# A macaron hybrid layer on one core: which blocks ask for a modulation column, how far behind the request its sum stands, and where readers of small transfers stand

## The chip, the cores and the metric

One of the eight cores of one Trainium2 chip runs the whole program. The metric is the device time of one execution in microseconds (us), as the median of several runs; lower is better. Beside it stands one execution taken by the hardware profiler. In its rows PE is TensorE (matmul), PEld its weight loads, DVE VectorE, ACT ScalarE, POOL GpSimd, and SP the engine whose queue (SPq) issues every DMA of this kernel. L140 is line 140 of the kernel before.

## The reference, cut

```
mod = silu(c) @ ada_w + ada_b                       # 9 x 2048 numbers: sh1, sc1, gt1, ... gt3
h = ada_in(x, norm_g[0], sh1, sc1);  x = x + 0.5 * gt1 * swiglu(h, gate[0], up[0], down[0])
h = ada_in(x, norm_g[1], sh2, sc2);  x = x + gt2 * hybrid_mixer(h, w_in, w_out, ...)
h = ada_in(x, norm_g[2], sh3, sc3);  x = x + 0.5 * gt3 * swiglu(h, gate[1], up[1], down[1])
return rmsnorm(x, final_norm)

def ada_in(x, g, shift, scale): return rmsnorm(x, g) * (1 + scale) + shift
def swiglu(h, wg, wu, wd):      return (silu(h @ wg) * (h @ wu)) @ wd
```

There are 256 tokens of width 2048 and a hidden width of 5632 = 44 x 128. The mixer has eight attention heads with a forget gate ("fox") and eight heads of a gated delta rule ("gdn") in chunks of 64, behind one input projection. Everything is float32.

## The kernel before, in words

**The weight stream.** All weights lie in device memory as 5392 tiles of 128x128, in the order in which the program uses them, eight to a block: 674 blocks of 512 KB, numbered 0 to 673. Each tile is used once. For each block `Stream.block` (L117) issues the DMA of `wraw` on SP (L125) and lets ACT copy it, rounded, to `whi` (L128); `Stream.next` (L130) lets DVE subtract to get `wlo` (L140). TensorE multiplies with both halves, so that a product is carried by two or three matmuls (L489/L490, L493/L494, L573 to L575). `whi` and `wlo` have four buffers each. `wraw` has four, and within the two feed-forward parts every fifth block goes to a fifth one (`more`), so that there the transfer of block b waits for the `wlo` of block b-5.

**The stages.** Blocks 0 to 111: gate and up products of the first 28 hidden chunks, in pieces (`gate_up_first`, L536); at the end of a chunk DVE adds two halves (L591, L592), multiplies (L524) and splits (L508). Blocks 112 to 167: the down products of those chunks, 3.5 blocks for each of 16 output chunks, with the residual on DVE (L517, L518). Blocks 168 to 231 and 232 to 263: the same for the other 16 hidden chunks. Blocks 264 to 409: the mixer. Blocks 410 to 673: the second feed-forward part.

**The columns.** `mod` has 144 columns of 128 numbers. For each, `ada_col` (L242) issues a DMA of 1 MB (`adat`, L261) placed behind the last `wraw` issue on SP, and DVE multiplies it with `silu(c)` and sums it up (L265; a column's sum, in the trace a custom instruction). `adat` has two buffers and, in the feed-forward parts, a third, so that column i waits for the sum of column i-3 there. The table `RATE` says how many columns each block asks for from a given block on; before, 0.2 in blocks 66 to 111, 0.5 in 112 to 167, 0.38 in 168 to 263, 0 in 264 to 283, 0.255 in 284 to 375, 0 in 376 to 423 and 0.16 after that.

**What sets the order.** Tile's scheduler decides at build time in which order an engine's instructions stand, by its own estimate of when each is ready; it moves an instruction ahead of others where it sees fit. `tc.issue_after(i)` (a pin) makes the instructions under it stand behind instruction i. Each engine then works through its row in that order, and a waiting instruction holds up all behind it. Where `W.late` holds (before: from the mixer on), a column's sum isn't written at once: it is kept in `W.owing`, and `settle` (L109) writes it in a later block under a pin behind that block's `wlo`, `BEHIND` = 2 blocks after the request. `ada_need` (L275), which makes sure that a column is there before it is read, writes all that is owed at once, with no pin. It is called for every tile of `gate_up_first` and once per output chunk in the residuals.

**Small transfers in the mixer.** `gates` stores 16 rows of cumulated gate values to device memory (`rowd`), and they are read back spread over all partitions: four rows at a time to `x<-rowd` (L921) for `decays` (L929, then eight exponentials L932), one row at a time to `rw<-rowd` (L897) for `decay` (`dec`, L908) and for `fox` (`fm`, L1174). `solve` sends blocks through device memory (L989 to L1012) and reads them at L1015 (`U0`). `keys` (L955) lets TensorE write `pk` and `pkk` (L961, L964), three buffers for both, of which `pk` is freed by the copy L968 on ACT and `pkk` by L974 on DVE, which needs the exponentials of L932.

## Time and profile before

| what | value |
|---|---|
| median of 3 runs | 1947.27 us (1946.34 to 1947.93) |
| profiled execution, its own time | 1948.17 us |
| its span, first to last instruction | 1946.4 us |
| PE busy | 1900.8 us, 98% of the span |
| DVE busy | 1558.7 us, 80% |
| ACT busy | 1040.3 us, 53% |
| mean granted TensorE clock | 0.994 |
| moved by DMA | 519.58 MB, mean 267 GB/s |

The profiled execution took 0.90 us more than the median of the runs; what is worked out from its rows is set against its own time, 1948.17 us. A busy PE is the bound of nearly all of the span, so that time can only come from the stretches where PE has no work and from those where its granted clock is below 1. Tables of stretches give, for each, the busy time and the instructions of each engine, the granted clock, the busy share of the DMA engines and GB/s.

### The profile page before, as it was taken

How to read it: one execution, taken by the hardware profiler on the slowest of the kernel's cores; microseconds unless marked ns; L12 is line 12 of the kernel's file. 1: busy time of each engine (PE TensorE's matmuls, PEld its weight loads, DVE VectorE, ACT ScalarE, POOL GpSimd, SP SyncE). 2: the span in 40 equal slices, each digit the busy share in tenths (PEclk: the TensorE clock that was granted, in tenths of full speed). 3: DMA queues.
4: the chain of work that ended last, by engine and by line, in shares of the span. 5: the costliest groups of instructions: out<-in, count | busy, mean ns of one | idle time of the engine just before them, and what ended most of it. 6: DMA issues, size and time to landing. Idle time of an engine off the chain costs nothing.

```text
span 1946.4 us, 33719 instructions
## 1 busy us (share of the span) xinstructions
PE 1900.8 (98%) x13086; PEld 1773.9 (91%) x13087; DVE 1558.7 (80%) x2414; ACT 1040.3 (53%) x1645; POOL 56.8 (3%) x55
## 2 busy tenths in 40 slices
PE   8999998999999999999999999999999999999998
PEld 7999998888899988899989999999999999999997
DVE  6999977999999997789987988877777666666654
ACT  7444544433444445857657656665554345554553
POOL 0000000000000021000000002000000000000011
PEclk9999999999999999999999999999999999999999
DMA  9998876999998885687667557677777666666663
GB/s 383 346 359 332 309 259 241 393 386 378 353 354 352 341 333 200 219 294 244 221 232 266 171 184 238 210 264 266 263 263 267 229 201 200 204 198 202 201 201 120
DMA packets 129490, 519.58 MB, mean 267 GB/s; under 512 B 18217, under 2 KB 21545, under 8 KB 111153
## 3 DMA queue, kind: packets, MB, share of 16 engines
q1 hardware_dynamic: 129330, 517.42, 74.0%
q8 instruction: 103, 1.69, 0.3%
q14 instruction: 57, 0.47, 0.1%
HBM read 512.89 MB, written 4.47 MB: 266 GB/s over the span
## 4 chain that ended last, share of the span: by engine, by line
PE 75%; DVE 11%; DMA 5%; issue 5%; ACT 3%; SPq 0%; DVEq 0%; ACTq 0%
PE pd L493 14%; PE pg L489 10%; PE pu L489 10%; PE pd L494 7%; PE pu L490 5%; PE pg L490 5%; DVE wlo L140 4%; PE po L493 3%; DMA adat<-in_ada_dram 2%; PE pgu L575 2%; PE pgu L573 2%; PE pgu L574 2%; PE pp L796 2%; PE pp L797 2%; PE pp L798 2%
## 5 line engine op out<-in xcount | busy, mean ns | idle before, releaser
L140 DVE TENSOR_TENSOR wlo<-wraw,whi 128x1024 fp32r<-128x1024 f32 x674 | 821.0, 1225 | 256.1 <-ACT whi L128 254.8
L128 ACT CAST whi<-wraw 128x1024 fp32r<-128x1024 f32 x674 | 698.9, 1046 | 504.4 <-PE pd L493 150.9
L493 PE MATMUL pd<-hid,whi 128*128 128x512 f32 x1408 | 462.0, 382 | 0.0
L494 PE MATMUL pd<-hid,wlo 128*128 128x256 f32 x1408 | 384.7, 273 | 4.8 <-DVE wlo L140 4.8
L265 DVE CUSTOM_DVE_ANT_0 adat<-adat,cs,colt 128x2048 f32<-128x2048 f32 x142 | 334.9, 2359 | 22.6 <-DMA adat<-in_ada_dram 22.6
L489 PE MATMUL pg<-hs,whi 128*128 128x512 f32 x912 | 302.3, 382 | 0.5 <-DVE shc L440 0.5
L489 PE MATMUL pu<-hs,whi 128*128 128x512 f32 x912 | 302.1, 382 | 0.0
L493 PEld LDWEIGHTS pd<-hid,whi 128*128 128x128 f32 x1408 | 266.0, 189 | 36.8
L494 PEld LDWEIGHTS pd<-hid,wlo 128*128 128x128 f32 x1408 | 270.2, 192 | 8.2 <-DVE wlo L140 8.0
L575 PE MATMUL pgu<-hs,wlo 128*128 128x256 f32 x896 | 240.6, 278 | 14.7 <-DVE wlo L140 14.3
L490 PE MATMUL pu<-hs,wlo 128*128 128x256 f32 x912 | 249.1, 273 | 0.0
L490 PE MATMUL pg<-hs,wlo 128*128 128x256 f32 x912 | 249.1, 273 | 0.0
L573 PE MATMUL pgu<-hs,whi 128*128 128x256 f32 x896 | 244.9, 277 | 0.4 <-ACT whi L128 0.3
L574 PE MATMUL pgu<-hs,whi 128*128 128x256 f32 x896 | 244.4, 276 | 0.0
L489 PEld LDWEIGHTS pg<-hs,whi 128*128 128x128 f32 x912 | 172.4, 189 | 24.8 <-ACT shc L439 0.7
L489 PEld LDWEIGHTS pu<-hs,whi 128*128 128x128 f32 x912 | 172.4, 189 | 23.7
L796 PE MATMUL pp<-hs,whi 128*128 128x256 f32 x656 | 188.9, 289 | 1.1 <-ACT hs L380 1.1
L575 PEld LDWEIGHTS pgu<-hs,wlo 128*128 128x128 f32 x896 | 168.4, 193 | 18.4 <-DVE wlo L140 18.3
L797 PE MATMUL pp<-hs,whi 128*128 128x256 f32 x656 | 182.4, 278 | 0.0
L798 PE MATMUL pp<-hs,wlo 128*128 128x256 f32 x656 | 181.9, 277 | 0.0
L490 PEld LDWEIGHTS pu<-hs,wlo 128*128 128x128 f32 x912 | 175.0, 192 | 1.0 <-DVE wlo L140 0.9
L490 PEld LDWEIGHTS pg<-hs,wlo 128*128 128x128 f32 x912 | 175.1, 192 | 0.6
(334 smaller groups left out, 2581.4 us busy)
## 6 DMA issues: line engine op xcount, KB each, us to landing
wraw<-in_w_dram SPq DMA_DIRECT2D x674, 512.0 KB, 4.5
adat<-in_ada_dram SPq DMA_DIRECT2D x142, 1024.0 KB, 7.5
xr<-in_xr_dram SPq DMA_DIRECT2D x4, 512.0 KB, 5.4
adaf<-in_ada_dram SPq DMA_DIRECT2D x4, 512.0 KB, 8.3
xd<-x SPq DMA_DIRECT2D x4, 512.0 KB, 7.4
rw<-rowd SPq DMA_DIRECT2D x16, 128.0 KB, 4.3
x<-xd SPq DMA_DIRECT2D x4, 512.0 KB, 5.3
out_dram<-o SPq DMA_DIRECT2D x8, 256.0 KB, 2.7
```

Of the source, the lines that this page charges most:

```text
L128: self.cast = self.nc.scalar.copy(self.h, r).ins
L140: lo_ = nc.vector.tensor_tensor(self.l, r, self.h.bitcast(F32), ALU.subtract)
L265: V.tensor_tensor_reduce(t, t, cs, 1.0, L("adab", q, 1), ALU.mult, ALU.add, mod[:, q : q + 1])
L489: PE.matmul(ps, wt[0], both, start=(k == 0), stop=False)
L490: PE.matmul(ps[:, T:], wt[1], part(k, HI), start=False, stop=(k == KD - 1))
L493: PE.matmul(ps, wt[0], act.rearrange("p q (a b) -> p q b a", a=2), start=first, stop=False)
L494: PE.matmul(ps[:, :T], wt[1], woven(act[:, 0]), start=False, stop=last)
L573: PE.matmul(o, wh, part(k, HI), start=first and s == 0, stop=False, skip_group_check=skip)
L574: PE.matmul(o, wh, part(k, LO), start=False, stop=False, skip_group_check=skip)
L575: PE.matmul(o, wl, part(k, HI), start=False, stop=last, skip_group_check=skip)
L796: PE.matmul(pp[i][:, :T], wh, hh, start=(k == 0), stop=False)
L797: PE.matmul(pp[i][:, :T], wh, hl, start=False, stop=False)
```

## The change

There are four parts:
- `RATE`: no column is asked for in blocks 90 to 111; 0.4 in place of 0.38 in blocks 168 to 263, and 0.285 in place of 0.255 in blocks 284 to 375.
- `W.late` holds from block 66 on (`LATE`), and the sum is settled three blocks after the request up to the mixer (`BEHIND[0]`), then two as before.
- `dec`, the first instruction of `decays`, and `U0` get a pin behind the `wlo` of the block that is current where they are written (`W.split`); the two `fm` instructions get one behind its cast (`W.cast`).
- `decays(1)` (the second four heads) is written 10 units of the planner's clock after it is due to start and not 5.

```diff
-RATE = (... (66, 0.2), (112, 0.5), (168, 0.38), (264, 0.0), (284, 0.255), (376, 0.0), (424, 0.16))
+RATE = (... (66, 0.2), (90, 0.0), (112, 0.5), (168, 0.4), (264, 0.0), (284, 0.285), (376, 0.0), (424, 0.16))
-BEHIND = 2
+BEHIND = (3, 2)
+LATE = 66
...
+            self.late = b >= LATE
...
             with self.tc.issue_after(lo_.ins):
-                self.settle(b - BEHIND)
+                self.settle(b - self.lag)
+            self.split = lo_.ins
...
-            V.tensor_tensor(dd, bc(C("mU")), gbv, ALU.add)
+            with tc.issue_after(W.split):
+                V.tensor_tensor(dd, bc(C("mU")), gbv, ALU.add)
...
-            yield 5.0
+            yield 10.0 if half else 5.0
...
-            V.tensor_tensor(Ln[:, hs4].rearrange("p h t j -> p (h t) j"), mL, rv, ALU.subtract)
+            with tc.issue_after(W.split):
+                V.tensor_tensor(Ln[:, hs4].rearrange("p h t j -> p (h t) j"), mL, rv, ALU.subtract)
...
             for q in range(2):
-                V.tensor_tensor(
+                with tc.issue_after(W.split):
+                    V.tensor_tensor(
...
-                A.activation(fm[:, o : o + wd], cb[:, :wd], AF.Identity, bias=colS[:, t, 0, h : h + 1], scale=-1.0)
+                with tc.issue_after(W.cast):
+                    A.activation(fm[:, o : o + wd], cb[:, :wd], AF.Identity, bias=colS[:, t, 0, h : h + 1], scale=-1.0)
...
-        W.late = True
+        W.lag = BEHIND[1]
```

**Where the columns stand now.** Counted in the order of SP and DVE of both kernels, block by block: in blocks 90 to 111 the kernel before asks for five columns (behind the transfers of blocks 90, 95, 100, 105 and 110), and the changed one for none. Blocks 112 to 167 have 28 in both. Blocks 168 to 263 have 34 before and 37 now, and blocks 264 to 375 have 24 before and 26 now. Before block 87 no column's request or sum has moved, although `W.late` holds from block 66 on: there `ada_need` settles what is owed before every pair of tiles. In blocks 112 to 167 most sums still stand in the block of their request, some one or two blocks later; from block 168 to 230 each stands three blocks later: the requests behind the transfers of blocks 168, 170, 173, 175 and 178 have their sums behind the `wlo` of blocks 171, 173, 176, 178 and 181, where before the requests of blocks 167, 170, 172, 175 and 178 had theirs behind the `wlo` of the same blocks.

DVE in blocks 91 to 95, first before (the first row is the `wlo` of block 91), then now (the rows of the same blocks).

```order
L140 TENSOR_TENSOR wlo<-wraw,whi 128x1024
L524 TENSOR_TENSOR tu<-tu,tg 128x256
L508 TENSOR_TENSOR hid<-tu,hid 128x256
L140 TENSOR_TENSOR wlo<-wraw,whi 128x1024
L265 ISA adat,mod<-adat,cs,colt 128x2048
L265 ISA mod 128x1
L591 TENSOR_TENSOR tg<-pgu,acc 128x256
L592 TENSOR_TENSOR tu<-pgu,acc 128x256
L140 TENSOR_TENSOR wlo<-wraw,whi 128x1024
L524 TENSOR_TENSOR tu<-tu,tg 128x256
L140 TENSOR_TENSOR wlo<-wraw,whi 128x1024
```

```order
L142 TENSOR_TENSOR wlo<-wraw,whi 128x1024
L527 TENSOR_TENSOR tu<-tu,tg 128x256
L511 TENSOR_TENSOR hid<-tu,hid 128x256
L142 TENSOR_TENSOR wlo<-wraw,whi 128x1024 x2
L594 TENSOR_TENSOR tg<-pgu,acc 128x256
L595 TENSOR_TENSOR tu<-pgu,acc 128x256
L527 TENSOR_TENSOR tu<-tu,tg 128x256
L142 TENSOR_TENSOR wlo<-wraw,whi 128x1024
L511 TENSOR_TENSOR hid<-tu,hid 128x256
L142 TENSOR_TENSOR wlo<-wraw,whi 128x1024
```

The sum (the rows ISA) that stood between `wlo` of block 92 and `wlo` of block 93 is gone, and the evacuation of a hidden chunk (tg, tu) stands one block further back. The sum's request stands behind the transfer of block 95 on SP, so that the sum stood three blocks ahead of the block of its own request.

SP where the mixer's rows come back, from the transfer of block 283 on, first before, then now.

```order
L883 DMA rowd<-x 8x512
L125 DMA wraw<-in_w_dram 128x1024
L261 DMA adat<-in_ada_dram 128x2048
L921 DMA x<-rowd 128x4x256
L897 DMA rw<-rowd 128x256 x2
L125 DMA wraw<-in_w_dram 128x1024 x4
L261 DMA adat<-in_ada_dram 128x2048
```

```order
L886 DMA rowd<-x 8x512
L126 DMA wraw<-in_w_dram 128x1024 x2
L925 DMA x<-rowd 128x4x256
L900 DMA rw<-rowd 128x256 x2
L126 DMA wraw<-in_w_dram 128x1024
L264 DMA adat<-in_ada_dram 128x2048
L126 DMA wraw<-in_w_dram 128x1024 x4
```

The read of the four rows (`x<-rowd`) has moved from behind the transfer of block 284 and a column's 1 MB to behind the transfer of block 285 with no column ahead of it.

ACT at the same place, from the cast of block 284 on, first before, then now.

```order
L128 CAST whi<-wraw 128x1024
L949 ACTIVATE kk<-cv 128x256
L1074 ACTIVATE kbd<-kk,colS 128x128
L1174 ACTIVATE fm<-rw,colS 128x128
L1174 ACTIVATE fm<-rw,colS 128x256
L945 COPY cp<-pp 128x256
L967 ACTIVATE j_9065,ssk<-pk 128x128
L932 ACT_TABLE_LOAD
L932 ACTIVATE Ln<-Ln,colS 128x128 x8
L967 ACTIVATE j_9067,ssk<-pk 128x128
L968 COPY kk<-pk 128x256
```

```order
L129 CAST whi<-wraw 128x1024
L1080 ACTIVATE kbd<-kk,colS 128x128
L937 ACT_TABLE_LOAD
L937 ACTIVATE Ln<-Ln,colS 128x128 x8
L954 ACT_TABLE_LOAD
L954 ACTIVATE kk<-cv 128x256
L972 ACTIVATE j_9059,ssk<-pk 128x128
L972 ACTIVATE j_9061,ssk<-pk 128x128
L973 COPY kk<-pk 128x256
L950 COPY cp<-pp 128x256
```

The two `fm` instructions no longer stand ahead of the eight exponentials `Ln`; they now stand behind the cast of block 302. On DVE the subtraction that feeds `Ln` (L929) has moved from behind `wlo` of block 284 to behind `wlo` of block 283, with three short instructions between, and `dec` from block 284 to block 305. From the cast of block 306 to that of block 307 ACT now has a table load, both `dec`, the fox exponentials, all eight `Ln`, a 384-wide copy, a convolution's first two steps and `rw`; before, the eight `Ln` stood behind the cast of block 304 and most of the others behind that of block 307.

More of the change, by code (lines that the diff above doesn't have):

```diff
@@ L34 @@
 NEG = -1e30
[L36 removed]
+RATE = ((0, 0.5), (28, 0.25), (33, 0.5), (49, 0.25), (56, 0.5), (66, 0.2), (90, 0.0), (112, 0.5), (168, 0.4), (264, 0.0), (284, 0.285), (376, 0.0), (424, 0.16))
 N_BIG, N_GDN = 3, 3
@@ L105, in __init__ @@
         self.lead = None
-        self.late, self.owing = False, []
+        self.late, self.owing, self.lag = False, [], BEHIND[0]
     def settle(self, upto=N_TILES):
@@ L1014, in solve @@
             for q in range(2):
-                V.tensor_tensor(
-                    U0[:, hs4].rearrange("p h t (b i) -> p (h t) b i", b=4)[:, 4 * q : 4 * q + 4],
-                    U[:, 4 * q : 4 * q + 4].unsqueeze(2).to_broadcast([P, 4, 4, 16]),
-                    C("blk").unsqueeze(1).unsqueeze(3).to_broadcast([P, 4, 4, 16]), ALU.mult)
+                with tc.issue_after(W.split):
+                    V.tensor_tensor(
+                        U0[:, hs4].rearrange("p h t (b i) -> p (h t) b i", b=4)[:, 4 * q : 4 * q + 4],
+                        U[:, 4 * q : 4 * q + 4].unsqueeze(2).to_broadcast([P, 4, 4, 16]),
+                        C("blk").unsqueeze(1).unsqueeze(3).to_broadcast([P, 4, 4, 16]), ALU.mult)
             if half == 0:
```

1 line of the change is left out of this document (removed).

## The prediction

> **What bounds the kernel now.** I read the page first, then the table of 20 us stretches, and in it looked only for stretches where PE is idle or its clock is below 1.
>
> ```profile
> PE 1900.8 (98%) x13086; PEld 1773.9 (91%) x13087; DVE 1558.7 (80%) x2414; ACT 1040.3 (53%) x1645; POOL 56.8 (3%) x55
> 260.00:280.00 20.00, 20.00 (x182) 20.00 (x181) 12.22 (x17) 8.65 (x11) 0.00 (x0) 1.00 0.70 255
> 280.00:300.00 20.00, 16.64 (x145) 16.26 (x143) 15.22 (x22) 7.70 (x12) 0.00 (x0) 0.98 0.56 194
> 300.00:320.00 20.00, 19.04 (x158) 18.85 (x158) 15.97 (x28) 10.35 (x17) 0.00 (x0) 0.93 0.68 235
> 320.00:340.00 20.00, 17.22 (x154) 17.03 (x153) 16.93 (x29) 10.64 (x17) 0.00 (x0) 1.00 0.72 261
> ```
>
> In each row: the stretch, its length, then busy us (instructions) of PE, PEld, DVE, ACT and POOL, the granted clock, the DMA share and GB/s. PE is the bound, with 1948.17 - 1900.8 = 47 us at most to win. Between 280 and 340 it has 3.36 + 0.96 + 2.78 = 7.1 us without work, while DVE is not full and the DMA engines are at 0.56 to 0.72: nothing there is short of capacity, so something waits for an order. The rows of PE with idle time ahead of them (in brackets, with what ended it) say for what:
>
> ```profile
> 283.21 0.38 PE L575 MATMUL pgu<-hs,wlo 128*128 128x256 f32 x1 [1.29 <-DVE wlo L140]
> 298.94 0.38 PE L575 MATMUL pgu<-hs,wlo 128*128 128x256 f32 x1 [2.07 <-DVE wlo L140]
> 315.19 0.38 PE L575 MATMUL pgu<-hs,wlo 128*128 128x256 f32 x1 [0.96 <-DVE wlo L140]
> 331.64 0.38 PE L575 MATMUL pgu<-hs,wlo 128*128 128x256 f32 x1 [2.78 <-DVE wlo L140]
> 344.16 0.38 PE L494 MATMUL pd<-hid,wlo 128*128 128x256 f32 x1 [1.54 <-DVE wlo L140]
> ```
>
> Five waits for `wlo`, 1.29 + 2.07 + 0.96 + 2.78 + 1.54 = 8.64 us. And DVE, in the rows that lead to the second one:
>
> ```profile
> 289.75 1.23 DVE L140 TENSOR_TENSOR wlo<-wraw,whi 128x1024 fp32r<-128x1024 f32 x1 [0.52 <-ACT whi L128]
> 294.73 2.35 DVE L265 CUSTOM_DVE_ANT_0 adat<-adat,cs,colt 128x2048 f32<-128x2048 f32 x1 [3.76 <-DMA adat<-in_ada_dram]
> 297.01 0.08 DVE L265 DVE_READ_ACCUMULATOR2_ANT mod<- 128x1 f32 x1
> 297.01 0.42 DVE L591 TENSOR_TENSOR tg<-pgu,acc 128x256 f32<-128x256 f32 x1
> 297.35 0.41 DVE L592 TENSOR_TENSOR tu<-pgu,acc 128x256 f32<-128x256 f32 x1
> 297.68 1.22 DVE L140 TENSOR_TENSOR wlo<-wraw,whi 128x1024 fp32r<-128x1024 f32 x1
> ```
>
> After a `wlo` DVE stands still for 3.76 us until the column's megabyte has landed, sums for 2.28 us (297.01 - 294.73), and only then does the evacuation and the next `wlo`, 7.9 us after the last one. The order puts the sum three blocks ahead of its own request's block; the request can't go out before the transfer that it stands behind gets a buffer, and the megabyte then takes 5.4 to 8.3 us:
>
> ```profile
>   DMA adat<-in_ada_dram: 10.3, 3
> DMA to landing us min/median/max: 5.4/7.9/8.3
> ```
>
> (of the columns between 285 and 345, where three of four sums waited).
>
> **The change part by part.**
>
> *No columns in blocks 90 to 111.* Five sums go from there with their waits. The first four gaps each follow one of them; the fifth follows the next column's sum, at 338.58 among the last evacuations, for which DVE had no lead left. Its place is now taken by a sum behind `wlo` of block 112, which DVE meets with its full lead. Without these sums DVE's load per block at its densest (a chunk of hidden values to 1 1/4 blocks, then to one) is a `wlo` of 1.22 us and 0.8 to 1 of a chunk's four short rows at 0.34 start to start, 2.3 to 2.6 us, where PE uses a block in 2.64 us (182 matmuls in 20 us in the row of 260, 24 to a block). So PE has nothing to wait for, though with little to spare over the last four blocks: -8.64 us, of which the last 1.54 may stay.
>
> *The clock.* PE's clock falls right behind the second gap:
>
> ```profile
> 294.00:300.00 6.00, 3.93 (x33) 3.74 (x31) 5.27 (x7) 1.16 (x3) 0.00 (x0) 0.95 0.32 127
> 300.00:310.00 10.00, 10.00 (x79) 10.00 (x79) 6.62 (x12) 6.31 (x9) 0.00 (x0) 0.86 0.86 299
> ```
>
> It costs 0.05 x 6 + 0.14 x 10 = 1.7 us. It begins at the end of a gap, so I let it go with the gap: -1.7 us. This is weaker: the longer gap at 331.64 has no such fall behind it (the row of 320 shows 1.00). [...]
>
> *The mixer's small readers.* One stop there follows from them:
>
> ```profile
> 812.58 0.80 ACT L1174 ACTIVATE fm<-rw,colS 128x128 f32<-128x128 f32 x2 [2.80 <-DMA rw<-rowd]
> 815.22 2.44 ACT L932 ACTIVATE Ln<-Ln,colS 128x128 f32<-128x128 f32 x8
> 816.35 0.44 PE L961 MATMUL pk<-colt,kk 128*128 128x128 f32 x2 [1.13 <-DVE Ln L974]
> 818.22 1.22 PE L964 MATMUL pkk<-kk 128*128 128x128 f32 x4 [1.22 <-ACT kk L968]
> 816.00:820.00 4.00, 2.43 (x9) 2.04 (x10) 2.17 (x10) 4.00 (x16) 0.00 (x0) 0.78 0.58 242
> 820.00:824.00 4.00, 4.00 (x16) 3.34 (x15) 4.00 (x9) 3.87 (x5) 0.00 (x0) 0.80 0.25 74
> ```
>
> ACT waits 2.80 us for a row of 128 KB whose `fm` nobody uses before block 302, and behind it stand the exponentials that free PE's buffers. With `fm` moved to block 302 the exponentials can begin some 3 us earlier. The subtraction ahead of them on DVE now stands behind `wlo` of block 283, and its data comes from a read issued at 802.1 and landed after 8.1 us:
>
> ```profile
> 802.14 0.43 SPq L921 DMA_DIRECT2D x<-rowd  x1
> DMA to landing us min/median/max: 8.1/8.1/8.1
> ```
>
> The order now puts no column of 1 MB ahead of that read, so that it lands at 810.2 or before; DVE may still wait for it a little, which the next `wlo` bears, since it stands some three blocks ahead of PE. The `pk` wait (1.13) then goes; of the `pkk` wait, which hangs on the copy behind a second table load, I keep 0.5. That is -1.85 us, bounds 0 and -2.35. The fall of the clock behind the stop, 0.22 x 4 + 0.20 x 4 = 1.7 us, I let go too.
>
> *Three columns more in blocks 168 to 263.* A sum takes 2.36 us of DVE:
>
> ```profile
> L265 DVE CUSTOM_DVE_ANT_0 adat<-adat,cs,colt 128x2048 f32<-128x2048 f32 x142 | 334.9, 2359 | 22.6 <-DMA adat<-in_ada_dram 22.6
> 345.00:430.00 85.00, 84.36 (x513) 76.80 (x512) 81.03 (x96) 35.96 (x37) 0.00 (x0) 1.00 0.99 395
> 430.00:505.00 75.00, 73.33 (x443) 66.36 (x442) 69.19 (x78) 26.74 (x28) 0.00 (x0) 1.00 0.97 372
> 505.00:590.00 85.00, 85.00 (x519) 77.89 (x518) 78.17 (x91) 42.93 (x65) 0.00 (x0) 1.00 0.93 356
> 680.00:700.00 20.00, 19.68 (x121) 17.85 (x120) 19.60 (x27) 8.61 (x12) 6.58 (x4) 1.00 0.86 339
> 700.00:720.00 20.00, 19.39 (x119) 17.56 (x118) 18.87 (x25) 9.07 (x12) 5.46 (x3) 1.00 0.97 374
> ```
>
> Blocks 168 to 231 run from about 500 to 670, with PE full, 6.8 us of 85 free on DVE and 7% free on the DMA engines: three sums of 7.1 us and 3 MB over 250 us hide there. The cover is gone in the down products (680 to 720), where PE already lost 0.32 + 0.61 = 0.93 us with about six columns (40 us, 2.6 a block, 0.38 a block), 0.16 a column: +0.5 us for three. Bounds 0 and +7.1 (nothing hidden). Blocks 112 to 167 (345 to 505) keep their 28 columns, the DMA at 0.97 to 0.99 and PE's loss of 0.64 + 1.67 = 2.3 us, which may go either way by that much.
>
> *Two columns more in blocks 284 to 375, and the other pins.* Between 860 and 1160 PE is without work for 300 - 292.82 = 7.2 us, in short stops behind chains through DVE and ACT:
>
> ```profile
> 860.00:1160.00 300.00, 292.82 (x2355) 280.98 (x2354) 257.82 (x636) 199.79 (x449) 0.43 (x2) 1.00 0.65 225
> L265 DVE CUSTOM_DVE_ANT_0 adat<-adat,cs,colt x20: 2335/2345/2349, 865.6 to 1136.3; 128x2048 f32<-128x2048 f32 x20
> ```
>
> If they all came of the 20 sums there, a sum would be worth 7.2 / 20 = 0.4: +0.8 us for two, bounds 0 and +4.7 (two sums of 2.35 in full). The other pins move readers further back; each new order of these chains may make or take single stops, -3 to +3 us, and I take 0.
>
> The sum: 1948.17 - 8.64 - 1.7 - 1.85 - 1.7 + 0.5 + 0.8 = 1935.6 us for an execution like the profiled one. That one stood 0.90 us above the median of its runs, so for the median 1934.7 us.
>
> **The rivals.**
>
> *The mixer keeps its stops.* ACT now has between the casts of blocks 306 and 307 the eight exponentials (2.44 us above), a table load of 1.28, and `dec`, the fox rows, the copy and the convolution at 0.4 to 0.5 each, some 8 us in all, where the lead of four `whi` buffers is about three blocks of 2.7 us less a cast and a `wlo`, 5.8 us (both are estimates from the rows of these groups). Where the stretch is not met by a full lead, PE waits for 2.2 us and more, and a stop at 816 that only shifts (1.85 + 1.7) comes on top: 1934.7 + 2.2 + 3.55 = 1940.5. For it speaks that the order has these rows in one piece; against it that PE has small matmuls of the attention in between, which stretch its blocks.
>
> *The clock falls anyway.* If the two falls don't come of the gaps, 3.4 us stay: 1938.1.
>
> *The held buffers starve the transfers: slower.* From block 168 to 230 a column's buffer is freed three blocks later. The request behind the transfer of block 175 needs the buffer of a column whose sum stands behind `wlo` of block 171, while that transfer itself went out after `wlo` of block 170: SP stands for a block and a sum, 2.6 + 2.3 us, and holds up all later transfers, on every second column, once in five blocks or 13 us. In those it must bring 5 x 0.524 + 2 x 1.049 = 4.7 MB. If the engines run dry for 2.5 us of each, the rest takes 4.7 MB in 10.5 us, 449 GB/s, and the trace never shows more than
>
> ```profile
> 20.00:40.00 20.00, 18.73 (x159) 18.09 (x160) 16.89 (x19) 14.92 (x26) 0.00 (x0) 1.00 1.02 423
> ```
>
> over 20 us. By 423 GB/s a cycle takes 11.1 + 2.5 = 13.6 us, 0.6 more than PE; at the 356 of this stage 15.7, 2.7 more. Twelve such cycles cost 8 to 33 us: at the upper end 1934.7 + 33 = 1968. It decides from the point at which nothing is left in flight while SP stands. Against it: when `wlo` is late, four transfers of blocks ahead are still in flight, over 5 us of work, so the engines don't run dry just when it matters, and 363 GB/s (4.7 in 13) is what the stage of 345 exceeded.
>
> *It doesn't do what it says.* The three blocks don't apply from 66 to 90, where the order hasn't changed, nor in most of blocks 112 to 167, where the residuals settle first. No gap of PE hangs on it (the row of 260 has PE at 20.00), so the time is that of the forecast.
>
> **How the numbers follow.** Forecast 0.60, mixer keeps its stops 0.16, clock falls anyway 0.10, starved transfers 0.10, better than 1929 (the 2.3 us of blocks 112 to 167 and half of the mixer's 7.2 go too) 0.04. The range of the forecast with its bounds: down 2.3 and 3, to about 1929; up with the rival of 1940.5 and a further 3 of the mixer's order, to 1944. A measurement of this kernel can tell about 0.2%, 3.9 us, from no change. Faster by more than that means below 1943.4: all cases but the starved one, 0.9; the starved one reaches from 1942.7 (8 us) to 1968: within the bound 0.03, slower 0.07.
>
> **What would show it.** Right: no gap of PE for `wlo` between 275 and 345, no wait of a sum for its megabyte there, the down products beginning some 10 us earlier, no clock below 1 from 290 to 310; at the second stop in the mixer no `pk` wait; SP waiting for a sum of DVE now and then from 490 to 660 with PE still full. Wrong: gaps for `wlo` there or in the down products of blocks 112 to 167, or a stretch of ACT at blocks 306 and 307 with PE idle behind it.

## The result and the profile after

| | median, us | range | runs |
|---|---|---|---|
| before | 1948.18 | 1945.38 to 1953.45 | 21 |
| after | 1950.92 | 1947.94 to 1953.33 | 21 |

The ratio is 1.0013, with a 95% interval of 1.0006 to 1.0020: the change made the kernel slower by a little over a tenth of a per cent. The forecast was 1934.7 us, in a range of 1929 to 1944. The profiled execution after took 1949.35 us, with a span of 1947.5 us (before: 1948.17 and 1946.4).

First the place that the forecast was about, in the same table of 20 us stretches, of the kernel after (stretch, length, then busy us and instructions of PE, PEld, DVE, ACT, POOL, the granted clock, the DMA share and GB/s):

```profile
280.00:300.00 20.00, 20.00 (x182) 20.00 (x181) 13.65 (x21) 9.40 (x14) 0.00 (x0) 1.00 0.59 193
300.00:320.00 20.00, 20.00 (x182) 20.00 (x181) 17.00 (x31) 11.99 (x19) 0.00 (x0) 1.00 0.61 207
320.00:340.00 20.00, 20.00 (x165) 19.55 (x164) 18.79 (x35) 11.72 (x20) 0.00 (x0) 1.00 0.85 318
```

The five gaps are gone, and so is the fall of the clock. So the gain came, and was given back elsewhere. Longer stretches of both kernels show where. Before:

```profile
420.00:500.00 80.00, 77.91 (x468) 70.16 (x467) 74.21 (x84) 28.34 (x27) 0.00 (x0) 1.00 0.98 377
500.00:660.00 160.00, 159.96 (x972) 146.16 (x971) 146.10 (x170) 81.34 (x122) 0.00 (x0) 1.00 0.91 353
660.00:740.00 80.00, 79.07 (x479) 71.79 (x478) 76.72 (x96) 38.39 (x51) 17.51 (x12) 1.00 0.86 318
780.00:860.00 80.00, 77.48 (x494) 70.63 (x493) 66.00 (x150) 59.41 (x107) 0.00 (x0) 0.98 0.69 243
```

After:

```profile
420.00:500.00 80.00, 74.70 (x441) 66.03 (x440) 67.51 (x79) 29.26 (x30) 0.00 (x0) 1.00 0.89 351
500.00:660.00 160.00, 156.27 (x940) 141.23 (x939) 140.63 (x165) 78.29 (x118) 0.00 (x0) 1.00 0.89 349
660.00:740.00 80.00, 76.34 (x452) 67.81 (x451) 78.72 (x97) 34.73 (x45) 16.76 (x11) 1.00 0.89 326
780.00:860.00 80.00, 79.52 (x529) 73.43 (x529) 63.92 (x146) 56.56 (x101) 0.00 (x0) 1.00 0.72 256
860.00:1160.00 300.00, 291.47 (x2339) 280.44 (x2338) 262.72 (x646) 202.67 (x454) 0.42 (x2) 0.99 0.64 231
```

PE is short of work by 5.3 us from 420 to 500 (before 2.1), by 3.7 from 500 to 660 (before 0.04) and by 3.7 from 660 to 740 (before 0.9). In the first two of these stretches DVE and the DMA engines do less than before, not more. From 780 to 860 the mixer's stop shrank as forecast, and of its two waits the one for `pk` is gone:

```profile
818.87 0.71 PE L969 MATMUL pkk<-kk 128*128 128x128 f32 x4 [0.48 <-ACT kk L973]
```

Since the kernels run apart by up to 20 us, stretches of equal time hold different blocks. So I cut each trace at the first matmul that reads the `wlo` of block 90, 112, 168 and 232, at the mixer's first `pp` matmul and at the first `po<-oh`. These are the stages of the profiled executions, in us; with them the medians of all kernels that ran, and the ratio of each to the kernel before as timed beside it, by which they are to be compared:

| kernel | median | ratio to before (95%) | to 90 | 90-111 | 112-167 | 168-231 | 232-263 | mixer | rest |
|---|---|---|---|---|---|---|---|---|---|
| before | 1948.18 | | 273.7 | 70.4 | 151.0 | 169.0 | 91.6 | 395.3 | 795.3 |
| after | 1950.92 | 1.0013 (1.0006-1.0020) | 275.5 | 59.0 | 152.9 | 176.8 | 95.2 | 392.8 | 795.2 |
| e1 no late sums | 1940.53 | 0.9955 (0.9943-0.9968) | 275.4 | 59.0 | 150.4 | 169.7 | 93.2 | 396.4 | 795.2 |
| e2 late sums only | 1954.87 | 1.0027 (1.0016-1.0039) | 275.4 | 68.5 | 153.2 | 171.2 | 92.4 | 397.0 | 795.6 |
| e3 rates only | 1941.65 | 0.9959 (0.9946-0.9972) | 275.7 | 59.0 | 150.4 | 169.8 | 93.2 | 394.2 | 795.8 |
| e4 mixer's pins only | 1944.54 | 0.9978 (0.9966-0.9989) | 274.9 | 68.0 | 151.0 | 169.0 | 91.6 | 391.2 | 795.8 |
| e5 one block late | 1952.77 | 1.0013 (1.0003-1.0022) | 275.4 | 59.0 | 151.4 | 180.0 | 94.4 | 396.6 | 795.2 |
| e6 two buffers | 1940.53 | 0.9947 (0.9935-0.9960) | 273.7 | 59.0 | 150.4 | 169.8 | 93.2 | 395.0 | 795.2 |
| e7 late to 167 | 1939.54 | 0.9946 (0.9933-0.9958) | 273.8 | 59.0 | 152.9 | 169.7 | 93.2 | 394.4 | 795.2 |
| e8 fewer in mixer | 1945.02 | 0.9972 (0.9960-0.9983) | 275.3 | 59.0 | 150.4 | 170.4 | 94.4 | 397.4 | 795.9 |
| e9 3 in 8 from 170 | 1939.32 | 0.9954 (0.9941-0.9967) | 275.3 | 59.0 | 152.9 | 167.7 | 91.8 | 394.8 | 795.9 |
| e10 3 in 8 from 172 | 1939.57 | 0.9951 (0.9939-0.9964) | 275.7 | 59.0 | 152.9 | 167.7 | 89.9 | 390.9 | 799.2 |
| e11 mixer's places | 1937.54 | 0.9945 (0.9932-0.9959) | 273.8 | 59.0 | 150.4 | 169.7 | 93.2 | 391.5 | 795.8 |
| e12 spread | 1935.25 | 0.9931 (0.9918-0.9944) | 274.7 | 59.0 | 150.4 | 170.4 | 90.0 | 391.1 | 798.0 |
| e13 two blocks late | 1936.74 | 0.9929 (0.9916-0.9941) | 273.6 | 59.0 | 147.1 | 169.8 | 93.9 | 394.3 | 795.2 |
| e14 rate 0.42 | 1951.80 | 1.0004 (0.9996-1.0013) | 275.8 | 59.0 | 152.9 | 177.3 | 96.2 | 391.4 | 797.5 |
| e15 shift by 4 | 1944.29 | 0.9973 (0.9963-0.9983) | 275.4 | 59.0 | 153.0 | 170.1 | 94.6 | 394.8 | 795.8 |
| e16 together | 1937.39 | 0.9933 (0.9921-0.9944) | 275.4 | 59.0 | 150.4 | 167.7 | 90.0 | 393.0 | 799.8 |
| e17 two late, places | 1935.48 | 0.9928 (0.9912-0.9943) | 275.8 | 59.0 | 147.4 | 169.8 | 93.8 | 392.5 | 796.5 |

The first two rows are the account of the change: +1.8 before block 90 (a fall of the clock to 0.50 from 107.5 to 110.9, the last section), -11.4 in the blocks without columns, +1.9, +7.8 and +3.6 in the blocks up to 263, -2.5 in the mixer; +1.1 in all, the difference of the spans after rounding. How far a single execution can be trusted differs by stage. Blocks 168 to 231 took 169.7 or 169.8 us in all five kernels in which these blocks have the same free sums (e1, e3, e6, e7, e11). The mixer has the same order, row for row, in the kernel after, e1, e5, e6, e7 and e13, and took from 392.8 to 396.6.

### The profile page after: what moved, and what is told of

Same layout as the page of the kernel before. It is cut to its first block, busy times and chain, and to the rows that moved or that the text cites. A ratio compares the mean times of both kernels' runs of the same rounds, so it can differ in the third digit from the quotient of the medians.

```text
span 1947.5 us, 33711 instructions
## 1 busy us (share of the span) xinstructions
PE 1903.0 (98%) x13086; PEld 1774.3 (91%) x13087; DVE 1556.8 (80%) x2414; ACT 1038.5 (53%) x1645; POOL 56.5 (3%) x55
## 4 chain that ended last, share of the span: by engine, by line
PE 69%; DVE 16%; DMA 5%; issue 4%; ACT 4%; SPq 0%; DVEq 0%; ACTq 0%
PE pd L496 12%; PE pg L492 9%; PE pu L492 8%; DVE wlo L142 6%; PE pd L497 6%; DVE adat L268 5%; PE pg L493 4%; PE pgu L578 4%; PE pu L493 4%; PE pgu L577 4%; PE pgu L576 4%; DMA wraw<-in_w_dram 4%; PE po L496 3%; PE pp L799 1%; ACT whi L129 1%
## 5 line engine op out<-in xcount | busy, mean ns | idle before, releaser
L492 PE MATMUL pg<-hs,whi 128*128 128x512 f32 x912 | 302.8, 382 | 0.5 <-DVE shc L443 0.5
```

The lines of the kernel that those rows point to most:

```text
L492: PE.matmul(ps, wt[0], both, start=(k == 0), stop=False)
```

## What the trace of after shows where the time went back

The first three of the five rows of PE between 500 and 660 in the kernel after that wait for more than 0.3 us:

```profile
527.37 0.38 PE L493 MATMUL pu<-hs,wlo 128*128 128x256 f32 x1 [0.85 <-DVE wlo L142]
...
554.51 0.38 PE L493 MATMUL pg<-hs,wlo 128*128 128x256 f32 x1 [0.52 <-DVE wlo L142]
...
582.24 0.38 PE L493 MATMUL pu<-hs,wlo 128*128 128x256 f32 x1 [0.86 <-DVE wlo L142]
```

The other two follow at 609.38 and 637.10, so they come every 27 us, ten blocks, and alternate: no accident, but a pattern of the order. DVE in the kernel after, ahead of the first of them:

```profile
518.46 1.21 DVE L142 TENSOR_TENSOR wlo<-wraw,whi 128x1024 fp32r<-128x1024 f32 x1
521.40 0.42 DVE L504 TENSOR_TENSOR tu<-pu,mg 128x256 f32<-128x256 f32 x1 [1.74 <-ACT mg L503]
521.86 0.43 DVE L527 TENSOR_TENSOR tu<-tu,tg 128x256 f32<-128x256 f32 x1
522.35 1.23 DVE L142 TENSOR_TENSOR wlo<-wraw,whi 128x1024 fp32r<-128x1024 f32 x1
523.49 0.42 DVE L511 TENSOR_TENSOR hid<-tu,hid 128x256 fp32r<-128x256 f32 x1
523.82 2.35 DVE L268 CUSTOM_DVE_ANT_0 adat<-adat,cs,colt 128x2048 f32<-128x2048 f32 x1
526.10 0.09 DVE L268 DVE_READ_ACCUMULATOR2_ANT mod<- 128x1 f32 x1
526.10 2.36 DVE L142 TENSOR_TENSOR wlo<-wraw,whi 128x1024 fp32r<-128x1024 f32 x2
```

The weights of block 180 are done at 519.67; then DVE stands 1.74 us until PE has finished the up half of its chunk (blocks 178 and 179) and ACT has copied it. At that moment PE has one block ahead, 180, some 2.6 us of work. Behind the evacuation come the weights of 181, which PE gets in time, and then the sum that the order pins three blocks past its request, 2.35 us, and only then the weights of 182: PE waits 0.85 us. (It costs more than the row shows: from the first `wlo` matmul of block 181 to that of 182 it takes 3.74 us, where a block without a wait takes 2.62, so 1.12. The row counts idle time only from the modelled end of the matmul ahead.) In the kernel before, the same weights and the same evacuation:

```profile
523.80 1.22 DVE L140 TENSOR_TENSOR wlo<-wraw,whi 128x1024 fp32r<-128x1024 f32 x1
524.93 2.35 DVE L265 CUSTOM_DVE_ANT_0 adat<-adat,cs,colt 128x2048 f32<-128x2048 f32 x1
...
527.21 0.42 DVE L501 TENSOR_TENSOR tu<-pu,mg 128x256 f32<-128x256 f32 x1
528.14 1.23 DVE L140 TENSOR_TENSOR wlo<-wraw,whi 128x1024 fp32r<-128x1024 f32 x1 [0.51 <-ACT whi L128]
```

There the sum, which nothing pins, stands ahead of the evacuation and fills the time in which DVE would wait for PE; behind the evacuation stand weights alone, those of 181 and, at 529.62, of 182.

## The experiments

The theories at the start: **A**, the late sums cost what the rest gains; **B**, the three columns more in blocks 168 to 263 cost it; **C**, a stream that is earlier at block 112 loses its lead there anyway.

**e1, no late sums.** The kernel after, with the sums placed freely up to the mixer:

```diff
-            self.late = b >= LATE
...
-        W.lag = BEHIND[1]
+        W.late, W.lag = True, BEHIND[1]
```

> The kernel after, but with the sums of blocks 66 to 263 placed freely as before (the late sums begin with the mixer, two blocks back, as before). Theory A (the pinned sums give the gain back: they cost 3.0 us in blocks 112 to 167, 3.7 in 168 to 231 and about 2 of the 2.7 in 232 to 263): about 9 us below the kernel after, 1941 to 1943, PE full from 500 to 660. Theory B (the columns put into blocks 168 to 263 cost it, free or pinned): within 3 us of the kernel after. Theory C (a stream that comes out of block 112 earlier runs into the transfers' limit and loses the lead again, whatever the order): within 3 us of the kernel after, with the loss in 345 to 505.

1940.53 us, ratio 0.9955 (0.9943 to 0.9968). Stages 112 to 263 took 413.3 us, 11.6 less than the 424.9 of the kernel after. The median is 0.5 below the 1941 to 1943 of A. A holds; B and C fall as the main cause.

**e2, late sums only**, on the kernel before (its `BEHIND`, `LATE` and lag, nothing else):

```diff
-BEHIND = 2
+BEHIND = (3, 2)
+LATE = 66
```

> The kernel before with only the pinned sums from block 66 on, three blocks past the request. Theory A: slower than before by some 8 us, lost between 410 and 740, the five gaps of 283 to 344 still there. Theories B and C: within 2 us of the kernel before.

1954.87, ratio 1.0027 (1.0016 to 1.0039), 6.4 us over the kernel before as timed beside it. The sign of A, and smaller than its 8: 2.2, 2.2 and 0.8 us in the three stages, 1.7 in the mixer. The same three blocks cost 7.1 us in blocks 168 to 231 of the kernel after and 2.2 here, so the lateness is not the price itself.

**e3, rates only** (the new `RATE` line on the kernel before):

```diff
-RATE = (... (66, 0.2), (112, 0.5), (168, 0.38), (264, 0.0), (284, 0.255), ...
+RATE = (... (66, 0.2), (90, 0.0), (112, 0.5), (168, 0.4), (264, 0.0), (284, 0.285), ...
```

> The kernel before with only the new table of rates (no columns in 90 to 111, three more in 168 to 263, two more in the mixer). Theory A: the five gaps go (-8.6, and the clock's 1.7 with them), the mixer's stop at 816 stays, 9 to 10 us below before. Theory B: 3 to 6 us are lost again in 500 to 740, 4 to 7 us below before. Theory C: no more than 3 us below before.

1941.65, 0.9959 (0.9946 to 0.9972), 6.9 us below the kernel before beside it: by the total that is the range of B (4 to 7), not that of A (9 to 10). The gaps went (70.4 to 59.0 us). The three columns cost 0.8 us in blocks 168 to 231 and 1.6 in 232 to 263, so B has a share of 2.4 us, less than the 3 to 6 that it had.

**e4, the mixer's pins only** (the kernel after with the rates of before and without late sums):

```diff
+            with tc.issue_after(W.split):
+                V.tensor_tensor(Ln[:, hs4].rearrange("p h t j -> p (h t) j"), mL, rv, ALU.subtract)
...
-            yield 5.0
+            yield 10.0 if half else 5.0
...
+                with tc.issue_after(W.cast):
+                    A.activation(fm[:, o : o + wd], cb[:, :wd], AF.Identity, bias=colS[:, t, 0, h : h + 1], scale=-1.0)
```

> The kernel before with only the mixer's pins and the later decays. If the part on the mixer was right (stop at 816 shortened by 1.85 us and the half clock behind it gone): 2 to 3.6 us below before. If the pins also bring the stop near 877 of the kernel after (1.93 us, and 1.8 of clock): the same as before.

1944.54, 0.9978 (0.9966 to 0.9989), 4.0 us below; the mixer took 391.2 instead of 395.3, and PE's rows show no wait from 790 to 830. Alone, this part of the forecast was right (what it does together with the new rates is said further down).

**What of a late sum costs?** A1: its place behind an evacuation. A2: the buffer that it holds, so that SP stands at the next column's request and the transfers behind it come late, the rival of the prediction.

**e5, one block late:**

```diff
-BEHIND = (3, 2)
+BEHIND = (0, 2)
```

> The kernel after with the sums of blocks 66 to 263 pinned one block past the request instead of three; the mixer is as in the kernel after. The buffers come free two blocks earlier, but the sums of 171, 181, 191 and so on to 231 still stand right behind an evacuation that waits for PE, as in the kernel after. Theory A1 (the place of the pinned sum costs): PE loses 3 to 5 us from 500 to 660 as in the kernel after, the whole within 4 us of it, 1947 to 1951. Theory A2 (the held buffers cost, through SP and late transfers): PE is full from 500 to 660, the whole near that without late sums, 1940 to 1942.

1952.77, 1.0013 (1.0003 to 1.0022), above the 1947 to 1951 of A1 and far from the 1940 to 1942 of A2, with the stage of 168 to 231 the longest of all, 180.0 us.

**e6, two buffers** instead of three for the columns of blocks 168 to 263, on e1:

```diff
-            t = (adap if W.more is None or i % 3 else W.more).tile([P, D], F32, name="adat")
+            t = (adap if W.more is None or i % 3 or len(W.order) >= 168 * WB else W.more).tile([P, D], F32, name="adat")
```

> The kernel without late sums of the first experiment, with two buffers for the columns instead of three from block 168 to 263, so that SP stands at a request until an earlier sum is done, while every engine's order is the same, row for row. Theory A1: the same as that kernel within 1 us, 1939.5 to 1941.5. Theory A2: the transfers behind the held request come late; 4 us and more above it, 1944 or more, lost from 500 to 740.

1940.53, the same as e1, with the same stage times from block 90 to 263. That SP did stand is in its waits (line, what ended the wait, us in all, times, longest), from 480 to 740. The kernel after, at a request (L264), its two largest, 93.4 us:

```profile
SPq L264 <- DVE mod L268: 70.9, 15, 7.0
SPq L264 <- DVE tu L504: 22.5, 6, 5.2
```

e6 at the same request (L263), its two largest, 64.0 us:

```profile
SPq L263 <- DVE mod L267: 42.4, 18, 3.3
SPq L263 <- DVE hid L510: 21.6, 6, 3.9
```

and e6's PE beside it, and below it that of e5, in which SP waits for no buffer of a column:

```profile
500.00:660.00 160.00, 159.89 (x967) 145.41 (x966) 147.51 (x171) 79.95 (x119) 0.00 (x0) 1.00 0.95 355
```

```profile
500.00:660.00 160.00, 154.22 (x920) 137.99 (x919) 139.33 (x161) 76.53 (x116) 0.00 (x0) 1.00 0.92 338
```

In e6 SP stands at the columns' requests for 64 us and more, and PE loses 0.1; in e5 it never stands there, and PE loses 5.8. The stands of e6 are shorter, 3.9 us at most against 7.0 in the kernel after. For those the waits of ACT, which casts what the transfers bring, decide. In blocks 168 to 231 of the kernel after these are all:

```profile
ACT mg L503 <- PE pg L493: 31.6, 16, 7.6
ACT mg L503 <- PE pu L493: 26.4, 16, 2.1
ACT tg L526 <- DVE tg L504: 19.1, 13, 2.4
ACT hid L510 <- DVE tu L527: 17.3, 12, 2.1
```

It waits for PE and for DVE, and not once for a transfer. A2 is out.

**e7, late sums only up to block 167:**

```diff
-            self.late = b >= LATE
+            self.late = LATE <= b < 168 or b >= 264
```

> The kernel after with late sums only from block 66 to 167 (and in the mixer, as before); free ones from 168 to 263. Theory A: the 3 us of 410 to 500 are lost as in the kernel after, with three sums in three blocks at 150 to 152 and 164 to 166, and PE is full from 500 to 660: 1943 to 1945. If blocks 112 to 167 lost their 3 us to something else than the late sums: 1940 to 1941.

1939.54, 0.9946 (0.9933 to 0.9958). Blocks 112 to 167 took 152.9 us as in the kernel after, 2.5 more than with free sums, and 168 to 231 the 169.7 of free ones. The stage costs what A expected. The total lies below both ranges (1943 to 1945 and 1940 to 1941): e7's profile took 1.6 us less than that of e1 ahead of block 90 (273.8 against 275.4), and its mixer, in the same order, took 2.0 us less than that of e1. What happens in these blocks is in DVE's rows of the kernel after:

```profile
437.78 2.35 DVE L268 CUSTOM_DVE_ANT_0 adat<-adat,cs,colt 128x2048 f32<-128x2048 f32 x1
...
440.45 1.21 DVE L142 TENSOR_TENSOR wlo<-wraw,whi 128x1024 fp32r<-128x1024 f32 x1
441.58 2.34 DVE L268 CUSTOM_DVE_ANT_0 adat<-adat,cs,colt 128x2048 f32<-128x2048 f32 x1
...
446.19 2.34 DVE L268 CUSTOM_DVE_ANT_0 adat<-adat,cs,colt 128x2048 f32<-128x2048 f32 x1
```

and PE's longest wait beside them:

```profile
441.72 0.38 PE L497 MATMUL pd<-hid,wlo 128*128 128x256 f32 x1 [0.91 <-DVE wlo L142]
```

A sum that is due three blocks later is called in early, when a residual needs its `gh`, together with the next ones: three sums in 10.8 us (437.78 to 448.5), behind one weight, one and two, with a row of the residual between: 3.8 us of DVE from the first sum to the second, where PE takes 2.6 for a block. The same happens once more at 477 to 485. At these two places PE's rows show 1.4 us of waits each, where e1 has 0.4 at blocks 149 to 153.

**e8, fewer columns in the mixer**, on e1:

```diff
-(168, 0.4), (264, 0.0), (284, 0.285)
+(168, 0.42), (264, 0.0), (284, 0.255)
```

> The kernel without late sums of the first experiment, with the rate 0.42 instead of 0.4 from block 168 and 0.255 instead of 0.285 in the mixer: two columns more before the mixer, three fewer in it. That kernel lost 13.2 us from 860 to 1160, where the kernel before lost 7.2. Theory M1 (the columns in the mixer cost it): 1935 to 1937, the loss of 860 to 1160 back at 7 to 9 us. Theory M2 (the order that the mixer's pins make costs it): 1939 to 1942. Should DVE have no room from 168 to 263 for two more sums: 1 to 3 us more on either, lost from 500 to 740.

1945.02, 0.9972 (0.9960 to 0.9983), far above the 1935 to 1937 of M1. The mixer took 397.4 us: M1 falls. Fewer columns did not help it.

**e9 and e10, late sums at fixed places.** At three columns in eight blocks the places repeat with the two chunks. On the kernel after, for e9 and e10:

```diff
-(168, 0.4), (264, 0.0)
+(168, 0.0), (170, 0.375), (264, 0.0)
```

```diff
-(168, 0.4), (264, 0.0)
+(168, 0.0), (172, 0.375), (264, 0.0)
```

> The kernel after, its late sums three blocks past the request kept, with a rate of three columns in eight blocks (0.375) from block 170 instead of 0.4 from 168, so that the sums keep their places in the eight blocks of two chunks: of the three, two stand ahead of an evacuation that waits for PE (behind the weights of blocks 181, 184 and so on) and one a block behind such an evacuation. 24 requests in blocks 168 to 231 instead of 26, two columns moved to later blocks. Theory A1 (what costs is a sum right behind an evacuation): the stage of blocks 168 to 231, 169.7 us with free sums and 176.8 in the kernel after, takes 169 to 172; the whole 1943 to 1946. Theory A3 (any sum three blocks late costs, wherever it stands): 175 and more, the whole about as the kernel after.

> The same as the kernel before this one, but from block 172: now all three sums of eight blocks stand right behind an evacuation that waits for PE (behind the weights of 183, 186, 188 and so on). 23 requests in blocks 168 to 231. Theory A1: 22 such places at 0.4 to 1.2 us each, 9 to 26 us over free sums, so that stage takes 178 to 195 us and the whole is the slowest of all. Theory A3: the same as the kernel before this one within 2 us.

1939.32 (0.9954, 0.9941 to 0.9967) and 1939.57 (0.9951, 0.9939 to 0.9964); blocks 168 to 231 took 167.7 us in both, less than with free sums (with 24 and 23 columns there instead of 26): 64 blocks of 2.62 us, without a wait. For e9 that is on A1's side, though below its 169 to 172; A3, which had 175 and more, falls. For e10 it is against A1: its sums do stand right behind evacuations and cost nothing. **A1 falls as I had put it.** e10's rows of DVE show what differs:

```profile
540.98 1.23 DVE L142 TENSOR_TENSOR wlo<-wraw,whi 128x1024 fp32r<-128x1024 f32 x1 [0.58 <-ACT whi L129]
542.12 0.42 DVE L504 TENSOR_TENSOR tu<-pu,mg 128x256 f32<-128x256 f32 x1
542.45 2.34 DVE L268 CUSTOM_DVE_ANT_0 adat<-adat,cs,colt 128x2048 f32<-128x2048 f32 x1
```

The evacuation finds its data ready: the order has put it three blocks or more behind the half chunk that it empties (the two blocks of a chunk's gate or up products), where the kernel after has it one behind. (Of the 32 evacuations of the stage, 27 stand three or four blocks behind in e10, none in the kernel after: there 17 stand one behind and 15 two.) So DVE, which does not wait for PE there, has its lead left when the sum comes. I counted, in the traces, for each evacuation of the stage its lead (the block of DVE's last weights less the last block of the half chunk) and whether a sum stands within the next two weights:

| kernel | lead 1 and a sum | PE's wait there, us | lead 1, no sum | lead 2 or more, with a sum | stage, us |
|---|---|---|---|---|---|
| before | 0 | 0 | 10 | 22 | 169.0 |
| e1 | 0 | 0 | 13 | 19 | 169.7 |
| e9 | 0 | 0 | 0 | 17 | 167.7 |
| e10 | 0 | 0 | 0 | 25 | 167.7 |
| e2 | 4 | 1.93 | 4 | 14 | 171.2 |
| e5 | 7 | 4.73 | 7 | 12 | 180.0 |
| after | 11 | 5.58 | 6 | 9 | 176.8 |

That is **A4**: a sum costs where the order lets DVE meet an evacuation with one block of lead and has the sum within the next two weights; the other two kinds of place cost little. e5 is the exception: with fewer such places than the kernel after it has the longest stage, and PE lost 2.5 us more where the lead was two and a sum stood behind it. So the count isn't all of the price. The number of columns in the stage is no rival: with 26 it took 169.7 us in e1 and 176.8 in the kernel after, with 27 170.4 in e8. A4 was formed on these rows; the next three kernels test it on orders that had not run.

**e13, e14, e15:** the kernel after, with one number of it changed each:

```diff
-BEHIND = (3, 2)
+BEHIND = (2, 2)
```

```diff
-(168, 0.4), (264, 0.0)
+(168, 0.42), (264, 0.0)
```

```diff
-(168, 0.4), (264, 0.0)
+(168, 0.0), (172, 0.4), (264, 0.0)
```

> The kernel after with the sums of blocks 66 to 263 two blocks past the request instead of three, and nothing else. Its order has 1 place in blocks 168 to 231 where an evacuation met with a lead of one block has a sum within the next two weights; the kernel after has 11. Theory A4 (such places cost, 0.65 us each over free sums): that stage takes 170 to 171 us, the whole 1941 to 1945 with what blocks 112 to 167 and 232 to 263 do. Theory A3 (late sums at a rate of 0.4 cost): 174 to 178 us.

> The kernel after with a rate of 0.42 from block 168 instead of 0.4. 13 such places, 27 requests in the stage. Theory A4: 178 to 180 us in blocks 168 to 231, the whole 1951 to 1956. If the count doesn't decide: anything from 168 to 177.

> The kernel after with its columns of rate 0.4 from block 172 instead of 168, so that 24 requests stand in the stage and 2 such places. Theory A4: 168 to 171 us in blocks 168 to 231. Theory A3: 174 to 178 us.

Blocks 168 to 231 took 169.8, 177.3 and 170.1 us, against 170 to 171, 178 to 180 and 168 to 171 by A4: e15 is inside, e13 0.2 and e14 0.7 us below, in the right order. A3's 174 to 178 missed twice, by 4 us. For e14 the other reading went up to 177, 0.3 below what was measured, so that e14 alone decides little. Totals: 1936.74 (0.9929, 0.9916 to 0.9941), 1951.80 (1.0004, 0.9996 to 1.0013) and 1944.29 (0.9973, 0.9963 to 0.9983); that of e13 is 4 us below its 1941 to 1945, since blocks 112 to 167 got shorter too. So two blocks instead of three turns the change from a loss into a gain of 13 us. DVE and PE of e13 at the same evacuation as above:

```profile
509.75 2.35 DVE L268 CUSTOM_DVE_ANT_0 adat<-adat,cs,colt 128x2048 f32<-128x2048 f32 x1
...
512.02 0.42 DVE L504 TENSOR_TENSOR tu<-pu,mg 128x256 f32<-128x256 f32 x1
```

```profile
410.00:480.00 70.00, 70.00 (x430) 64.33 (x428) 65.78 (x74) 27.29 (x26) 0.00 (x0) 1.00 0.99 401
480.00:650.00 170.00, 170.00 (x1027) 154.43 (x1026) 156.76 (x180) 84.27 (x127) 0.00 (x0) 1.00 0.95 354
```

The sum is back ahead of the evacuation, and PE is full, in blocks 112 to 167 too (147.1 us, the shortest). There most sums now stand in pairs behind the same weights; why that costs less than free sums (150.4) was not looked into.

**e11 and e12, the mixer's columns** at the places that they have in e4, on e1; e12 also moves one out of 232 to 263:

```diff
-(284, 0.285), (376, 0.0)
+(284, 0.835), (285, 0.255), (360, 0.385), (376, 0.0)
```

```diff
-(168, 0.4), (264, 0.0), (284, 0.285), (376, 0.0)
+(168, 0.42), (232, 0.35), (264, 0.0), (284, 0.905), (285, 0.255), (360, 0.385), (376, 0.0)
```

> The kernel without late sums of the first experiment, with the columns of the mixer at the places that they have in the kernel with the pins alone (every fourth block from 284), and the two that are more at its end, from 360 on. The mixer took 391.2 us with the pins alone and 396.4 with pins and the columns at a rate of 0.285 (395.0 and 394.4 in two other kernels of that order). Theory M3 (the mixer's stops hang on where its columns stand against its pinned readers): 391 to 393 us in it, the whole 1935 to 1938. Theory M2 (they vary from one order to the next without a cause that can be set): 394 to 397, the whole 1940.

> The same as the kernel before this one, with a column moved from blocks 232 to 263 (11 there took 93.2 us, 10 took 91.6) to 168 to 231 (27 there took 170.4 us, 26 took 169.7): 0.5 to 1.5 us below the kernel before this one if a column costs what the stages say, the same if not.

1937.54 (0.9945, 0.9932 to 0.9959) and 1935.25 (0.9931, 0.9918 to 0.9944). The mixer took 391.5 and 391.1 us, against 394.4 to 396.4 in three kernels with the columns of e1 (e1, e6, e7). That is the range of M3, but it isn't shown: the kernel after has the order of e1 in the mixer and took 392.8, and by the ratios e11 isn't told apart from e1 or e6. e12 is 2.3 us below e11 by the medians, more than expected, and by the profiled spans the same (1933.5): the 3.2 us that it gains in 232 to 263 are paid back by 0.7 in 168 to 231, 2.2 in the rest and 0.9 ahead of block 90.

**e16 and e17, put together.** e16 is e10 with `self.late = b >= 168`; e17 is e13 with the mixer's rates of e11.

> What cost nothing, together: the tenth kernel (three columns in eight blocks from 172, late; 167.7 us in blocks 168 to 231, 89.9 in 232 to 263, 390.9 in the mixer), with free sums ahead of block 168 (150.4 us in blocks 112 to 167 instead of 152.9). 2.5 us below the tenth kernel, 1936 to 1938, faster than before by 0.5 to 0.6 per cent.

> The kernel with sums two blocks late, with the columns of the mixer at the places of the kernel with the pins alone. If stages add up: 147.1 us in blocks 112 to 167, 169.8 in 168 to 231, 391 to 393 in the mixer, the whole 1933 to 1935, the fastest of all. If the mixer's time is chance: 394 to 397 there, the whole as the kernel with sums two blocks late alone, 1936 to 1938.

1937.39 (0.9933, 0.9921 to 0.9944), inside its range, and 1935.48 (0.9928, 0.9912 to 0.9943), 0.5 above its 1933 to 1935. e16's stages are as expected up to block 263, but the rest took 799.8 us: with 23 and 10 columns ahead of the mixer, the order has four requests at blocks 403 to 409, where a modulation needs them, and blocks 403 to 417 took 4 us longer than in e1. e17 is faster than the kernel before and the kernel after, and no better than e13 within the interval; its mixer, 392.5 us, is 1.8 below e13's, less than the mixer of one order varies.

## Why the prediction was wrong, point by point

- **The five gaps, -8.64: right; the clock's 1.7: right for this execution, by luck.** Blocks 90 to 111 took 11.4 us less, in e3 alone too; the last gap of 1.54 went with the others. The fall of the clock was not the order's: e4 keeps the order of before in these blocks, with 7.8 us of PE idle, and its clock stays at 1.00 (68.0 us instead of 70.4).
- **The mixer's stop, -1.85 and 1.7: the stop is right, the sum for the mixer is luck.** The `pk` wait went and 0.48 us of the other stayed, where I kept 0.5. PE's loss from 780 to 860 fell by 79.52 - 77.48 = 2.04 us and the clock rose from 0.98 to 1.00 of 80 us. With the two columns (+0.8) the forecast for the mixer was -2.75; its stage took 2.5 us less in this one execution; the same order took from 2.5 us less to 1.3 more than before in the six executions named above. And a part of the rival came too, unpriced in the forecast. ACT and PE of the kernel after, at the casts of blocks 306 and 307:

```profile
874.27 1.05 ACT L129 CAST whi<-wraw 128x1024 fp32r<-128x1024 f32 x1 [0.79 <-DMA wraw<-in_w_dram]
875.34 1.28 ACT L914 ACT_TABLE_LOAD   x1
```

```profile
877.48 0.33 PE L1201 MATMUL ppt<-colt,x 128*128 128x128 f32 x1 [1.93 <-ACT x L1196]
```

  The stretch is there, from 875.3 to the next cast at 883.1, and PE waits 1.93 us in it, not for a cast, as the rival had it, but for the row `x` behind the table load and `dec`; behind it the clock is at 0.50 from 878.9 to 882.3. The pins alone took 4.0 us off (e4). With the new rates they took off next to nothing: e1, with pins, and e3, without, have ratios of 0.9955 and 0.9959. The 3 us either way that I gave to orders cover that.
- **Three columns in blocks 168 to 263, +0.5: too small.** e1 and e3 measured +0.7 or 0.8 and +1.6, so 2.4 us, within the bounds of 0 and 7.1. The term that was too small is the price of a column: 0.8 us instead of 0.16. The loss of 0.16 us a column that I took from 680 to 720 was an average over sums with and without a wait behind them.
- **The step that failed is the price of nothing for the late sums themselves.** The prediction had them in two places: in blocks 112 to 167, where the residuals would settle them and the time "may go either way" by 2.3 us, and in 168 to 263, where the only cost that I gave them was the buffer that they hold. The first costs 2.5 us (e7): at two places sums that are called in come three in three blocks, and PE waits behind them. The second costs 7.1 us in 168 to 231 and 2.0 in 232 to 263 (after against e1), and not for the buffer: SP stands just as the prediction said, but no transfer comes late for it in the kernel after, and e6 with its shorter stands loses nothing. What I left out is what a pin does on its own engine. A sum that may go anywhere is put by the order where DVE waits for PE; pinned behind the weights of a given block it stands where the count of blocks puts it, and 11 times that is where DVE has one block of lead. I had DVE's 6.8 us free of 85 as cover, which is an average: in the rows of before, 3.1 us of it are waits ahead of evacuations and 2.5 waits for a cast, and the pin took sums out of the first.
- The slower rival had the sign for that part, and the wrong mechanism; its condition, nothing left in flight while SP stands, is not what decides.
- **What stays open:** how the order comes to put an evacuation one, two or four blocks behind its half chunk was only counted; A4 doesn't give the 180.0 us of e5; why the late sums cost 2.0 us in 232 to 263 was not looked into; nor what makes the mixer's 391 or 396, in one order or between two.

## What to carry to other kernels

A wait that is taken out of an order is cheap to forecast; work that is pinned is not free merely because its engine has slack on average: find, at the very place where it will stand, how much lead the engine has there, and whether it just waited for the engine that it feeds. A place inside a wait is worth keeping: here a sum of 2.35 us that lost it cost some 0.65 us of PE, (176.8 - 169.7) / 11. And where a change has parts, one of them can hide the gain of the rest: here two blocks instead of three made a ratio of 1.0013 into 0.9929.

## What the runs showed of the clock

The prediction tied a fall of PE's clock to the gap ahead of it and could not say why the gap of 2.78 us at 331.64 has none. The kernel after shows the same from the other side: up to block 86 the order of its DVE and ACT is that of before, PE waits 2.72 us at 106.78 as it does at 106.61 before, and here the clock falls to 0.50 and there it stays at 1.00. Rows of 3.4 us, before:

```profile
101.40:104.80 3.40, 2.49 (x23) 2.30 (x21) 3.40 (x7) 0.51 (x1) 0.00 (x0) 1.00 0.70 281
104.80:108.20 3.40, 1.58 (x14) 1.59 (x15) 3.40 (x6) 1.37 (x2) 0.00 (x0) 1.00 0.18 42
108.20:111.60 3.40, 3.40 (x33) 3.40 (x32) 3.40 (x3) 1.38 (x2) 0.00 (x0) 1.00 0.89 307
```

After:

```profile
104.10:107.50 3.40, 0.72 (x6) 0.72 (x7) 3.40 (x6) 1.88 (x3) 0.00 (x0) 1.00 0.02 4
107.50:110.90 3.40, 3.40 (x18) 3.40 (x18) 3.40 (x4) 1.04 (x1) 0.00 (x0) 0.50 0.80 240
```

Between 30 and 1900 us, and outside the modulation at 730 to 763, the clock is at 0.50 in the profile of the kernel after from 107.5 to 110.9 and from 878.9 to 882.3, behind 3.4 us in which PE was idle for 2.68 and 1.93 us; in that of the kernel before from 299.4 to 302.8 and from 818.2 to 821.6, behind 3.4 us with 2.07 and 2.33. By an estimate from these rows one such stretch costs 0.50 x 3.4 = 1.7 us of PE's work. The length of a stop doesn't tell by itself where that happens: of the two waits of 2.72 us one has a fall behind it and one has none, and before, PE was idle for 2.74 us from 328.2 to 331.6 and the clock stayed at 1.00 from 331.6 to 338.4. What decides it was not shown. That the falls make the spread between executions isn't shown either: of the 21 runs of the kernel after, the seven with a mean clock of 0.994 took 1949.31 to 1952.19 us and the four with 0.996 took 1947.94 to 1951.10.
